# Windowed attention: low and high values side by side in one 512-column product

## The chip, the cores and the metric

The kernel runs on one core of one Trainium2 chip. The metric is device time in microseconds (us) of one execution. A profile of one execution shows every instruction of TensorE (PE, with its weight loads as PEld), VectorE (DVE), ScalarE (ACT), GpSimd (POOL) and the DMA queues.

## What is computed

The reference is an encoder trunk of two layers on 256 tokens of width 1024. Each layer is a feed-forward block, a mixer, and a second feed-forward block, each followed by a layer norm. The first layer's mixer is an mLSTM, the second's is the windowed attention that the change touches. Cut to what matters:

```
p = x @ w_in                              # 16 query heads, 4 key/value heads of 64
s = einsum('bnqkgd,bnskd->bnkgqs', q, kw) * (64 ** -0.5) - slopes * dist
s = where(valid, s, MASK_VALUE)           # |t - s| <= 128
m = maximum(max(s), sink)
pe = exp(s - m)
attn = pe / (sum(pe) + exp(sink - m))
o = einsum('bnkgqs,bnskd->bnqkgd', attn, vw)
return o @ w_out
```

Four query heads share one key/value head.

## The kernel before

**Stages.** Six stages follow each other: feed-forward, mLSTM, feed-forward, feed-forward, attention, feed-forward (`trunk_kernel`). All products are made from split numbers: each operand is written as a high part (rounded for TensorE, dtype `FR`) and a low part (what is left), and a product is high x high + high x low + low x high (`mm3`, line 617). `split_evac` (line 636) takes a result from PSUM in this way: ScalarE copies the high part, VectorE subtracts it from the result for the low part. Weights go the same road: `Weights.high` (ScalarE, `w_hi`) and `Weights.low` (VectorE, `w_lo`) split each piece of 128x1024; TensorE can use a piece only when both are done.

**Order.** The order of work is written out by hand (`manual_schedule`): each engine does its instructions in the order in which the program names them. `Paced` (line 65) wraps the engines and keeps modelled clocks (`pe`, `vec`, `act`); in the feed-forward stages a filler uses these clocks to choose where weight splits are put. In the attention there is no filler: `W.done(..., PU[st], True)` at line 1580 puts a fixed number of `w_hi` into each step (`PU` = 2, 1, 2, 1, 1, 0, 1, 2 for steps 3 to 10), and `W.lows()` at line 1584 the `w_lo` belonging to them.

**PSUM.** Two sets of four banks: `wbank` (name `pw`) and `ybank` (name `py`). A bank holds 128 x 512 numbers of 32 bits. A new `pw` tile takes the bank of the tile used longest ago, when all its readers are done.

**Attention** (`attn`, line 1335). Queries, keys and values are projected first; `qT`, `kT` hold transposed queries and keys, `va[t]` the values of 128 tokens. Then a loop of eleven steps `st` (line 1552) is a pipeline over eight pairs of heads j; pair j's two heads a = 0, 1 share one key/value head. In step st stand, in this order:

- `values(st - 3)` (line 1504): the sum of values weighted by probabilities, transposed: 128 rows (head a in rows 64a to 64a+63) by 256 queries. The result's high and low parts replace the queries in `qT[:, j]` (lines 1559, 1560; tiles `q_hi`, `q_lo`). In the prediction these two are d0 and d1.
- `rest` (two short exps `es` on ScalarE) and `scale(st - 1)` (line 1479): GpSimd divides pair st - 1's probabilities by their sums.
- a first part of the filling matmuls `work` (`FB[st]` of them): parts of the query projection in steps 0 to 3, of the output projection in steps 4 to 10.
- `turn(st - 2, 0, p0)` (line 1492): TensorE transposes pair st - 2's probabilities for the first 128 keys; ScalarE copies the high part (`pr`).
- `W.done`: the step's `w_hi` on ScalarE.
- `scores(st)` (line 1437), up to step 7: TensorE's scores; VectorE's four reductions (`sc`, with row minimum `nm`), with the low part of `pr` of the first 128 keys after the second; then `late`, which is `turn(st - 2, 1, p1)` for the other 128 keys; then four exps on ScalarE.
- `flush(2)`: the low part of the second `pr`; `W.lows()`: the step's `w_lo`, both on VectorE; and the rest of `work` on TensorE.

**values before.** `va[sb]` has five columns of 64 per key/value head: zeros, high, zeros, low, zeros. Twelve matmuls of 256 columns add up in a 128 x 256 result: for both blocks of keys sb and both heads a, (high values, high probabilities), (low, high), (high, low). The window `at` of 128 columns puts the values into the rows of head a and zeros into the other head's.

After the loop, `tail` (line 716) finishes the output projection; its first matmuls use chunk 7 of `qT`, which is `values(7)`.

Of the kernel before, what the change touches and what calls it, by code (L numbers as in the profile page):

```python
# [9 lines left out]
F32 = mybir.dt.float32  # L10
FR = mybir.dt.float32r
# [6 lines left out]
S = 256  # L18
# [170 lines left out]
class Weights:  # L189
# [134 lines left out]
    def low(self):  # L324

        nc = self.nc
        i, hi = self.half.pop(0)
        p = self.plan[i]
        k, scale, raw = p["k"], p["scale"], self.raw[p["word"]]
        lo = self.pool.tile([128, D], FR, name="w_lo", tag="w_lo", bufs=RING)  # L330
        if i == 0:
            for j in range(2):
                s_ = slice(j * 512, j * 512 + 512)
                nc.vector.tensor_sub(lo[:, s_], raw[:, s_], hi[:, s_].bitcast(F32))
        elif scale is None:
            nc.vector.tensor_sub(lo, raw, hi.bitcast(F32))
        else:
            nc.vector.scalar_tensor_tensor(lo, raw, scale(), hi.bitcast(F32), op0=OP.mult, op1=OP.subtract)
        self.parts[i] = (hi.rearrange("p (k f) -> p k f", k=k), lo.rearrange("p (k f) -> p k f", k=k))
        self.fresh = i  # L340
        sums = [(i, *sum_) for sum_ in self.after.get(i, ())]
        while sums and not isinstance(sums[0][2], int):
            self.transfer(*sums.pop(0)[1:])
        self.sums += sums
        self.drop(p["word"])
        self.load()
# [98 lines left out]
def trunk_kernel(ctx: ExitStack, tc: tile.TileContext, x, ffn_w_in, ffn_w_out, ln_g, ln_b, ml_w_in, ml_gate_b,  # L445
                 ml_norm_g, ml_w_out, at_w_in, at_sink, at_w_out, out):
    nc = Paced(tc.nc)
# [169 lines left out]
    def mm3(o, l, r, start, stop, onto=False):  # L617
        nc.tensor.matmul(o, l[0], r[0], start=start, stop=False, skip_group_check=onto)
        nc.tensor.matmul(o, l[0], r[1], start=False, stop=False, skip_group_check=onto)
        nc.tensor.matmul(o, l[1], r[0], start=False, stop=stop, skip_group_check=onto)  # L620

    def pair(p, *idx):
        return p[0][idx], p[1][idx]

    def wbank(shape=(128, 512)):
        return psum.tile(list(shape), F32, name="pw", tag="pw", bufs=4)
# [6 lines left out]
    def tok(t):  # L633
        return slice(t * 128, (t + 1) * 128)

    def split_evac(dst, src, scale=None, high=None, wait=False):
        if scale is None:
            (high or nc.scalar.copy)(dst[0], src)
            low = lambda: nc.vector.tensor_sub(dst[1], src, dst[0].bitcast(F32))
            if wait:  # L640
                W.when_ready(low, dst[0])
            else:
                low()
        else:
            nc.scalar.activation(dst[0], src, AF.Copy, scale=scale)
            nc.vector.scalar_tensor_tensor(dst[1], src, scale, dst[0].bitcast(F32), op0=OP.mult, op1=OP.subtract)
# [688 lines left out]
    def attn(l, n, pending, last):  # L1335
        with ExitStack() as ph:
            pool = ph.enter_context(tc.tile_pool(name="attn", bufs=1))
            tile_ = lambda shape, dt, name, **kw: pool.tile(shape, dt, name=name, tag=kw.pop("tag", name), **kw)

            def both(shape, name, bufs=1):  # L1340
                return tuple(tile_(shape, FR, name + e, bufs=bufs) for e in ("_hi", "_lo"))
# [24 lines left out]
                                        base=128, channel_multiplier=-sign)  # L1366
            dist = tile_([128, 2, S], F32, "dist")
            nc.gpsimd.tensor_add(dist, fwd, back)
            va = [tile_([128, 4, 5, 64], FR, f"v{t}") for t in range(2)]
            for t in range(2):  # L1370
                nc.gpsimd.memset(va[t][:, :, 0:5:2].bitcast(F32), 0.0)
            qT = both([128, 8, S], "q")
            kd, qd = [], []

# [2 lines left out]
            def proj(t, m):  # L1377
                ps = wbank()
                for k in range(8):
                    if t == 0 and m == 1 and k == PEND[bound[0] - 1]:  # L1380
                        pending()
                        W.done(0, PD[bound[0] - 1])
                    if 4 * m + k // 2 == len(pieces):
                        pieces.extend(W.take(1))
                    mm3(ps, pair(xT, A, k, tok(t)), pair(pieces[4 * m + k // 2], A, k % 2), k == 0, k == 7)
                    if t == 1 and k % 2:
                        W.done(W.used - 8 + 4 * m + k // 2 + 1, 1 if m == 0 and k < 4 else 0)
                if m == 0:
                    kv = ps.rearrange("p (a g d) -> p a g d", a=2, g=4)
                    kk = tile_([128, 4, 2, 64], F32, "kd", tag="sc", bufs=6)  # L1390
                    nc.scalar.copy(kk, kv[:, 0, :, None, :].to_broadcast([128, 4, 2, 64]))
                    split_evac((va[t][:, :, 1], va[t][:, :, 3]), kv[:, 1])
                    kd.append(kk)
                else:
                    qq = tile_([128, 4, 128], F32, "qd", tag="sc", bufs=6)
                    nc.vector.tensor_mul(qq.rearrange("p j (a d) -> p (j a) d", a=2),
                                         ps.rearrange("p (h d) -> p h d", h=8),
                                         qs_row[:, :, None].to_broadcast([128, 8, 64]))
                    qd.append(qq)
# [27 lines left out]
            sc, pr = {}, {}  # L1427
# [74 lines left out]
            lows, sums = [], {}  # L1502

            def values(j):
                p = wbank((128, S))
                terms = [(sb, a, e, f) for sb in range(2) for e, f in ((0, 0), (1, 0), (0, 1)) for a in range(2)]
                for n_, (sb, a, e, f) in enumerate(terms):
                    v = va[sb][:, j // 2].rearrange("p s d -> p (s d)")
                    at = 128 * e + 64 * (1 - a)
                    nc.tensor.matmul(p, v[:, at:at + 128], pr[j, sb][f][:, a], start=n_ == 0, stop=n_ == len(terms) - 1)  # L1510
                sums[j] = p
                for sb in range(2):
                    del pr[j, sb]
                    W.back(TAGS[2 + sb], 1)
# [17 lines left out]
            def parts(f_, *args):  # L1532
# [3 lines left out]
                return [lambda t=t, o=o: out_part(args[0], t, o) for t in args[1] for o in range(2)]  # L1536

            proj(0, 0)
            proj(0, 1)
            nc.scalar.preload_act_table(AF.Exp)  # L1540
            proj(1, 0)
            k_turn(0)
            q_turn(0)
# [8 lines left out]
            for st in range(11):  # L1552
                if st == 2:
                    gb = load_ln(lambda name: tile_([128, D], F32, name), l, n)
                if 0 <= st - 3 < 8:
                    values(st - 3)
                    o = sums.pop(st - 3)
                    d = pair(qT, A, st - 3)
                    nc.scalar.copy(d[0], o)
                    nc.vector.tensor_sub(d[1], o, d[0].bitcast(F32))  # L1560
# [36 lines left out]
    for j, (kind, l, i, n) in enumerate(stages):  # L1597
        last = j == len(stages) - 1
        bound[0] = j
        nc.filler = W.fill if kind == "ffn" else None  # L1600
        if kind == "ffn":
            pending = ffn(l, i, n, pending, last)
        elif kind == "mlstm":
            pending = mlstm(l, n, pending, last)
        else:
            pending = attn(l, n, pending, last)
# [29 lines left out]
```

## Time and profile before

| what | us |
|---|---|
| runs of the kernel before, median of 3 | 914.19 |
| lowest and highest | 912.9, 914.21 |
| span of the profiled execution, first to last instruction | 911.7 |
| median of the runs less that span | 2.5 |
| TensorE busy in the profiled execution | 902.5 |
| attention's steps 3 to 10, first `values` to last | 681.1 to 717.7 |

Of the profiled execution, the span is what the record holds; the median of the runs stands beside it. The profile is read in views: the page with its summary (busy times, the chain of work that ended last); stretches, which give for a window of time each engine's busy time, with the number of instructions, then the granted TensorE clock (1.00 is full speed), the DMA share and GB/s; the instructions in order of time (start, duration, engine, line, operation, output<-inputs, count, and in brackets how long the engine stood idle before and what ended it); groups of equal instructions (busy time in us, mean ns of one, idle time before them); and the view of one tile with what waited for it. Nearly all instructions pass through line 180, where `Paced` calls the engine, so they are told apart by tiles. Durations of neighbours overlap a little; the distance from start to start tells what an instruction costs its engine.

### The profile page before, as it was taken

How to read it: one execution, taken by the hardware profiler on the slowest of the kernel's cores; microseconds unless marked ns; L12 is line 12 of the kernel's file. 1: busy time of each engine (PE TensorE's matmuls, PEld its weight loads, DVE VectorE, ACT ScalarE, POOL GpSimd, SP SyncE). 2: the span in 40 equal slices, each digit the busy share in tenths (PEclk: the TensorE clock that was granted, in tenths of full speed). 3: DMA queues.
4: the chain of work that ended last, by engine and by line, in shares of the span. 5: the costliest groups of instructions: out<-in, count | busy, mean ns of one | idle time of the engine just before them, and what ended most of it. 6: DMA issues, size and time to landing. Idle time of an engine off the chain costs nothing.

```text
span 911.7 us, 12563 instructions
## 1 busy us (share of the span) xinstructions
PE 902.5 (99%) x4459; PEld 757.4 (83%) x4459; DVE 804.4 (88%) x971; ACT 573.1 (63%) x793; POOL 152.5 (17%) x192
## 2 busy tenths in 40 slices
PE   9999999999999999999999999999999999999996
PEld 7888888889988888888888888888898888888885
DVE  5999999886799898999888899998869889899886
ACT  5776777356664656776646676764569566676660
POOL 0111123113211011212011111110425301111110
PEclk9999999999999999999999999999999999999999
DMA  8999998546637898997868989986534587899851
GB/s 281 367 328 259 288 274 215 162 137 186 208 111 246 296 234 244 290 285 234 241 193 269 259 257 283 272 223 197 159 119 140 163 293 221 204 298 278 252 138 47
DMA packets 100703, 208.53 MB, mean 229 GB/s; under 512 B 6904, under 2 KB 21264, under 8 KB 100640
## 3 DMA queue, kind: packets, MB, share of 16 engines
q1 hardware_dynamic: 82368, 173.04, 54.2%
q0 software_dynamic: 17696, 33.65, 22.3%
q10 hardware_dynamic: 576, 1.05, 0.3%
q8 instruction: 35, 0.57, 0.3%
q14 instruction: 28, 0.23, 0.1%
HBM read 206.65 MB, written 1.05 MB: 228 GB/s over the span
## 4 chain that ended last, share of the span: by engine, by line
PE 98%; DVE 1%; DMA 0%; issue 0%; DVEq 0%
PE pw L180 64%; PE py L180 35%; DMA x<-in_x_dram 0%; DVE x L180 0%; DVE stats L180 0%; DVEq L1632 0%; DVE mv L180 0%; DVE rs L180 0%
## 5 line engine op out<-in xcount | busy, mean ns | idle before, releaser
L180 DVE TENSOR_TENSOR w_lo<-w_raw,w_hi 128x1024 fp32r<-128x1024 f32 (+1 forms) x213 | 255.2, 1219 | 26.6 <-ACT w_hi L180 24.8
L180 ACT CAST w_hi<-w_raw 128x1024 fp32r<-128x1024 f32 (+1 forms) x213 | 218.9, 1049 | 80.3 <-PE py L180 21.7
L180 DVE TENSOR_TENSOR w_lo<-s_raw,w_hi 128x1024 fp32r<-128x1024 f32 x192 | 228.6, 1219 | 18.3 <-ACT w_hi L180 18.2
L180 ACT CAST w_hi<-s_raw 128x1024 fp32r<-128x1024 f32 x192 | 196.6, 1054 | 58.4 <-PE py L180 23.3
L180 PE MATMUL pw<-w_hi,xT_hi 128*128 128x512 f32 x480 | 189.5, 396 | 0.0
L180 PE MATMUL pw<-w_hi,xT_lo 128*128 128x512 f32 x480 | 187.0, 391 | 0.0
L180 PE MATMUL pw<-w_lo,xT_hi 128*128 128x512 f32 x480 | 186.7, 390 | 0.0
L122 POOL DMA_DIRECT2D s_raw<-in_ffn_w_in_dram x64 | 77.4, 1211 | 484.1 <-DVE s_raw L180 226.3
L180 PE MATMUL py<-w_hi,h_hi 128*128 128x512 f32 x349 | 138.2, 396 | 0.0
L180 PE MATMUL py<-w_hi,h_lo 128*128 128x512 f32 x349 | 136.2, 390 | 0.0
L180 PE MATMUL py<-w_lo,h_hi 128*128 128x512 f32 x349 | 136.0, 390 | 0.0
L180 PEld LDWEIGHTS pw<-w_hi,xT_lo 128*128 128x128 f32 x480 | 90.0, 188 | 19.1
L180 PEld LDWEIGHTS pw<-w_lo,xT_hi 128*128 128x128 f32 x480 | 90.3, 188 | 18.6 <-DVE w_lo L180 1.2
L180 PEld LDWEIGHTS pw<-w_hi,xT_hi 128*128 128x128 f32 x480 | 90.1, 188 | 17.4 <-ACT w_hi L180 0.2
L180 PE MATMUL pw<-w_hi,S_hi 128*128 128x512 f32 x256 | 99.7, 390 | 0.0
L180 PE MATMUL pw<-w_lo,S_hi 128*128 128x512 f32 x256 | 99.7, 389 | 0.0
L180 PE MATMUL pw<-w_hi,S_lo 128*128 128x512 f32 x256 | 99.7, 389 | 0.0
L180 PEld LDWEIGHTS py<-w_hi,h_lo 128*128 128x128 f32 x349 | 65.5, 188 | 14.1
L180 DVE TENSOR_TENSOR s_raw<-s_raw,s_raw 128x1024 f32<-128x1024 f32 x64 | 76.8, 1219 | 0.3
L180 PEld LDWEIGHTS py<-w_lo,h_hi 128*128 128x128 f32 x349 | 65.7, 188 | 13.0
L180 PEld LDWEIGHTS py<-w_hi,h_hi 128*128 128x128 f32 x349 | 65.6, 188 | 12.7
L180 PEld LDWEIGHTS pw<-w_hi,S_lo 128*128 128x128 f32 x256 | 48.1, 188 | 10.0
(205 smaller groups left out, 1122.7 us busy)
## 6 DMA issues: line engine op xcount, KB each, us to landing
s_raw<-in_ffn_w_in_dram SPq DMA_DIRECT2D x96, 512.0 KB, 8.0
w_raw<-in_ffn_w_out_dram SPq DMA_DIRECT2D x88, 512.0 KB, 6.1
w_raw<-in_ffn_w_in_dram SPq DMA_DIRECT2D x64, 512.0 KB, 5.7
s_raw<-in_ffn_w_in_dram POOLq DMA_DIRECT2D x64, 512.0 KB, 8.3
w_raw<-in_ml_w_in_dram SPq DMA_DIRECT2D x24, 512.0 KB, 4.6
w_raw<-in_ffn_w_in_dram SPq DMA_DIRECT2D x32, 256.0 KB, 6.0
w_raw<-in_at_w_in_dram SPq DMA_DIRECT2D x12, 512.0 KB, 4.8
w_raw<-in_ml_w_out_dram SPq DMA_DIRECT2D x8, 512.0 KB, 4.1
```

The costliest lines, as they stand in the source:

```text
L122: self.nc.gpsimd.dma_start(ap, source, accum_op=OP.add)
L180: r = f(out, *args, **kw)
```

## The change

The values' columns are ordered low, high, zeros (three columns of 64 in place of five). A window of 128 columns from column 0 then holds low and high values side by side, and from column 64 high values and zeros. Each of the four matmuls has both heads' probabilities as its 512 columns: (low and high) with the high probabilities, (high and zeros) with the low probabilities, for two blocks of keys. The result is 128 x (2 heads x 256): rows 0 to 63 hold low x high + high x low, rows 64 to 127 hold high x high. Behind the matmuls, for each head, ScalarE copies the upper half into a new tile `o` and VectorE adds the lower half to it (for head 1 the halves change roles). In the prediction these four are c0, a0, c1, a1. d0 and d1 then read `o` in SBUF instead of PSUM.

```diff
-            va = [tile_([128, 4, 5, 64], FR, f"v{t}") for t in range(2)]
+            va = [tile_([128, 4, 3, 64], FR, f"v{t}") for t in range(2)]
             for t in range(2):
-                nc.gpsimd.memset(va[t][:, :, 0:5:2].bitcast(F32), 0.0)
+                nc.gpsimd.memset(va[t][:, :, 2].bitcast(F32), 0.0)
...
-                    split_evac((va[t][:, :, 1], va[t][:, :, 3]), kv[:, 1])
+                    split_evac((va[t][:, :, 1], va[t][:, :, 0]), kv[:, 1])
...
             def values(j):
-                p = wbank((128, S))
-                terms = [(sb, a, e, f) for sb in range(2) for e, f in ((0, 0), (1, 0), (0, 1)) for a in range(2)]
-                for n_, (sb, a, e, f) in enumerate(terms):
+                p = wbank((128, 2, S))
+                terms = [(sb, f) for sb in range(2) for f in range(2)]
+                for n_, (sb, f) in enumerate(terms):
                     v = va[sb][:, j // 2].rearrange("p s d -> p (s d)")
-                    at = 128 * e + 64 * (1 - a)
-                    nc.tensor.matmul(p, v[:, at:at + 128], pr[j, sb][f][:, a], start=n_ == 0, stop=n_ == len(terms) - 1)
-                sums[j] = p
+                    nc.tensor.matmul(p, v[:, 64 * f:64 * f + 128], pr[j, sb][f], start=n_ == 0, stop=n_ == len(terms) - 1)
+                o = tile_([128, S], F32, "o", bufs=2)
+                for a in range(2):
+                    r = slice(64 * a, 64 * a + 64)
+                    nc.scalar.copy(o[r], p[64 - 64 * a:128 - 64 * a, a])
+                    nc.vector.tensor_add(o[r], o[r], p[r, a])
+                sums[j] = o
```

## The prediction

> **What bounds the kernel now.** I read the page's busy line and its chain first, then the stretches of the attention stage, then that stage's instructions in order of time, engine by engine.
>
> ```profile
> PE 902.5 (99%) x4459; PEld 757.4 (83%) x4459; DVE 804.4 (88%) x971; ACT 573.1 (63%) x793; POOL 152.5 (17%) x192
> ...
> PE 98%; DVE 1%; DMA 0%; issue 0%; DVEq 0%
> ```
>
> TensorE is the bound of the whole: the chain that ended last runs on it for 98%. But these are averages over six stages, and the change lies in one. Two of the attention's eleven steps (step 4 and step 7 of the loop at line 1552), by the busy times of stretches (PE, PEld, DVE, ACT, POOL, clock):
>
> ```profile
> 685.96:691.50 5.54, 5.54 (x42) 4.66 (x41) 4.94 (x12) 5.32 (x17) 2.77 (x6) 1.00 0.32 106
> ...
> 702.50:708.00 5.50, 5.50 (x42) 4.67 (x41) 5.00 (x15) 4.87 (x16) 3.19 (x8) 1.00 0.54 171
> ```
>
> Here ScalarE is busy 4.87 to 5.32 and VectorE 4.94 to 5.00 of some 5.5 us: the three engines run level. ScalarE's 63% is the other stages' number. So the attention has almost no cover for more work on these two, and this decides the forecast.
>
> **The change, part by part: TensorE.** In the order of time, start and duration in us:
>
> ```profile
> 501.03 5.44 PE py L180 x24
> ```
>
> ```profile
> 681.10 1.60 PE L180 MATMUL pw<-pr,v 128*128 128x256 f32 x12
> 682.54 0.60 PE L180 MATMUL pw<-ident,sc 128*128 128x128 f32 x4
> ...
> 705.14 0.60 PE L180 MATMUL pw<-ident,sc 128*128 128x128 f32 x4
> 705.68 0.39 PE L180 MATMUL pw<-kT_hi,q_hi 64*128 64x256 f32 x2
> ...
> 706.59 0.66 PE L180 MATMUL pw<-ident,sc 128*128 128x128 f32 x4
> ...
> 708.47 1.80 PE L180 MATMUL pw<-pr,v 128*128 128x256 f32 x12
> ```
>
> The twelve matmuls of values took 682.54 - 681.10 = 1.44 us. Of 512 columns, 24 took 5.44, so 0.227 each and four 0.91. The change takes 0.53 us from TensorE per pair of heads, 8 x 0.53 = 4.2 us in all. That is the whole possible gain.
>
> **ScalarE and VectorE.** The result of values(j) now passes six instructions in a row where it passed two. Before: high copy d0, low subtraction d1. After: copy c0, add a0, copy c1, add a1, then d0, d1. Both engines work strictly in the order written, so each waits for the other with everything of its step queued behind. Step 7 before, on ScalarE and then on VectorE:
>
> ```profile
> 705.67 0.35 ACT L180 CAST q_hi<-pw 128x256 fp32r<-128x256 f32 x1
> 705.93 0.48 ACT L180 ACTIVATE es<-nm,sink 128x2 f32<-128x2 f32 x2
> 706.31 0.57 ACT L180 CAST pr<-pw 128x512 fp32r<-128x512 f32 x1
> 706.78 1.05 ACT L180 CAST w_hi<-w_raw 128x1024 fp32r<-128x1024 f32 x1
> 707.73 0.58 ACT L180 CAST pr<-pw 128x512 fp32r<-128x512 f32 x1
> ...
> 709.65 0.49 ACT L180 ACTIVATE sc<-sc,nm 128x256 f32<-128x256 f32 x1
> ...
> 710.14 0.50 ACT L180 ACTIVATE sc<-sc,nm 128x256 f32<-128x256 f32 x1
> ```
>
> ```profile
> 683.57 0.41 DVE L180 TENSOR_TENSOR q_lo<-pw,q_hi 128x256 fp32r<-128x256 f32 x1
> ...
> 689.53 0.48 DVE L180 SCALAR_TENSOR_TENSOR q_lo<-py,qs_col,q_hi 128x256 fp32r<-128x256 f32 x1
> 689.92 0.41 DVE L180 TENSOR_TENSOR q_lo<-pw,q_hi 128x256 fp32r<-128x256 f32 x1
> ...
> 695.00 0.43 DVE L180 TENSOR_TENSOR q_lo<-pw,q_hi 128x256 fp32r<-128x256 f32 x1 [0.18 <-ACT q_hi L180]
> ...
> 701.10 0.42 DVE L180 TENSOR_TENSOR q_lo<-pw,q_hi 128x256 fp32r<-128x256 f32 x1
> ...
> 706.05 0.42 DVE L180 TENSOR_TENSOR q_lo<-pw,q_hi 128x256 fp32r<-128x256 f32 x1 [0.18 <-ACT q_hi L180]
> 706.80 0.48 DVE L180 CUSTOM_DVE_ANT_0 sc<-pw,dist,neg_sink 128x256 f32<-128x256 f32 x1 [0.32 <-POOL sm L1485]
> ...
> 707.61 0.69 DVE L180 TENSOR_TENSOR pr<-pw,pr 128x512 fp32r<-128x512 f32 x1
> ...
> 709.02 0.69 DVE L180 TENSOR_TENSOR pr<-pw,pr 128x512 fp32r<-128x512 f32 x1
> 709.62 1.22 DVE L180 TENSOR_TENSOR w_lo<-w_raw,w_hi 128x1024 fp32r<-128x1024 f32 x1
> ...
> 711.02 0.43 DVE L180 TENSOR_TENSOR q_lo<-pw,q_hi 128x256 fp32r<-128x256 f32 x1 [0.18 <-ACT q_hi L180]
> ...
> 714.52 0.42 DVE L180 TENSOR_TENSOR q_lo<-pw,q_hi 128x256 fp32r<-128x256 f32 x1 [1.12 <-ACT q_hi L180]
> ```
>
> From start to start: d0 0.26, both es 0.38, a pr cast 0.47, w_hi 0.95, an exp 0.49; on VectorE two score reductions 0.81, a pr low part 0.60, w_lo 1.22 less the same overlap of 0.09, so 1.13. From one engine's end to the other's start 0.03 (705.67 + 0.35 to 706.05); I count 0.04.
>
> The new operations have no row, so they get bounds:
>
> ```profile
> L180 ACT CAST S_hi<-S 128x512 fp32r<-128x512 f32 x16 | 10.0, 623 | 15.2 <-DVE S L180 15.1
> ...
> L180 DVE DVE_READ_ACCUMULATOR2_ANT nm<- 128x1 f32 x32 | 2.7, 83 | 0.0
> ...
> L180 DVE TENSOR_TENSOR wt<-pw,wt 128x256 f32<-128x256 f32 x4 | 1.7, 414 | 0.0
> ```
>
> A copy of 64 partitions x 256 from PSUM lies between nothing and the 0.623 of 512 columns; I take 0.36, the q_hi cast of 256 columns. An add of 64 x 256 lies between 0 and 0.69 (512 columns); I take 0.42, the wt row with PSUM and SBUF in. d0 now reads SBUF: 0.35 to 0.62, I take 0.38; d1 stays 0.42.
>
> May c1 run while a0 runs? They touch other columns of one PSUM bank and other halves of o. The mLSTM stage has the same case: line by line, VectorE copies ucol from a bank and ScalarE reads ecol from its other columns, with nothing else between them.
>
> ```profile
> L180 ACT ACTIVATE ecol<-pw x1: 278/278/278, 213.5 to 213.5; 128x128 f32<-128x128 f32 x1
> its engine sat idle before it (us, times) until:
>   DVE ucol L180: 1.7, 1
> ```
>
> ScalarE stood idle until VectorE had read: the two are made to take turns on a bank. So I put c1 behind a0. [...]
>
> Count a step from a0's start, with one weight piece: a0 ends 0.42, c1 0.46 to 0.82, a1 0.86 to 1.28, d0 1.32 to 1.70, d1 from 1.74. ScalarE is free at 1.32 + 0.26 = 1.58 (before, 0.12 ahead of d1's start), VectorE at 1.74 + 0.33 = 2.07 (a 256-column subtraction by the 512 and 1024 ones: 0.60 - 0.27). Then VectorE: reductions to 2.88, pr low to 3.48, reductions to 4.29, pr low to 4.89, w_lo to 6.02. ScalarE: es 1.96, pr 2.43, w_hi 3.38, pr 3.85, first exp 4.34; the second waits for the last reduction's read-out (0.08) and hand-over, to 4.41, so three exps to 5.88, the next c0 to 6.24, next a0 at **6.28**. Before, step 7 took 711.02 - 706.05 = 4.97. With two pieces (steps 3, 5) the second pr cast ends 0.95 later, its low part runs 4.95 to 5.55, two w_lo to **7.81**, against 701.10 - 695.00 = 6.10.
>
> Start of a0 after, against d1's start before: step 3 683.57, the same. Step 3 has the two-piece 7.81 and one q_lo of a query projection more (0.39), so step 4 begins 691.77 (+1.85). Step 5: 698.05 (+3.05). Step 6: 705.86 (+4.76). Step 7: 712.14 (+6.09). Step 8: 718.42 (+7.40). Steps 8 and 9 have no scores: es and two pr casts, low parts ending at 3.87; the last matmul of values, which reads the second low part, is written 0.45 later (0.06 and 0.39, the duration of one of 512 columns); c0 at 4.35, a0 at 4.75, so step 9 at 723.17 (+8.65). There es is missing, but a w_hi follows the casts to 3.57 and its w_lo, to 4.74, stands in front of a0: step 10 at 727.91.
>
> TensorE covers none of it. Its own work of such a step is values 0.91, first transposes 0.54, scores 0.91, second transposes and output projection 708.47 - 706.59 = 1.88: 4.24, under 6.28; its last values matmul waits for the low part of the step before. The values bank goes to the second transposes (line 1575), which now wait for a1 (1.34) instead of d1; they are wanted by ScalarE only at 3.38. GpSimd's scaling follows es; it is busy 3.19 in step 7's stretch, so from 2.1 it ends about 5.3, and the transposes that read it come in the next step, whose reductions start at 6.28 + 2.07. No DMA moves; the smaller memset (POOL, line 1371) lies long before.
>
> ```profile
> 718.51 0.42 DVE L180 TENSOR_TENSOR q_lo<-pw,q_hi 128x256 fp32r<-128x256 f32 x1
> ```
>
> ```profile
> 719.12 0.39 PE L180 MATMUL py<-w_hi,q_hi 128*128 128x512 f32 x1
> ```
>
> After step 10 the output projection's tail begins with chunk 7, at 719.12 before. It needs d0: 727.91 + 1.70 + 0.06 = 729.67. **TensorE is 10.5 us late**, and from there to the end it has no gap to win any back. Span 911.7 + 10.5 = 922.2. The median of the runs is 914.19, 2.5 above the profiled span; with that, **924.7 us**.
>
> **The rivals.**
>
> *All is hidden, faster.* If ScalarE and VectorE took the six instructions in their idle time, TensorE would keep its 4.2: 914.19 - 4.2 = 910.0. The 98% chain speaks for it. The point from which it decides is the room of step 7: its two-engine loop before is by the same count 4.56 of 4.97 (0.33 + 0.81 + 0.60 + 0.81, 0.12 to the exps, 3 x 0.49, d0 and hand-over 0.42), so 0.4 us, and the change lengthens it by 1.7. 5%.
>
> *c1 beside a0.* If the two reads are allowed together, d0 starts at 0.79 rather than 1.32. Eight steps x 0.53 = 4.2 less: 920.5. For it: they read different columns and write different halves of o. Against: the ecol row, where that was so too. 10%.
>
> *The following stage is planned anew.* Paced (line 65) counts the changed instructions in its own clocks, and in the last feed-forward stage these choose when a w_hi or w_lo is written. One pair misplaced costs at most its 1.05 + 1.22 = 2.3 us where TensorE runs gapless: 925 to 929. 6%.
>
> *The clock drops.* TensorE would stand some 2 us of each step. Its clock was 1.00 in both stretches above, but there it never stood. At half clock its 4.24 would be 8.48, 2.2 over the step, and 1.5 over in the light ones: 5 x 2.2 + 3 x 1.5 = 15.5 more, 940. [...] 4%.
>
> **How the numbers follow.** Forecast 74%, with its own 922.5 to 927.0: the new operations' bounds, nearest rows taken, are worth some 0.25 us a step either way, 2 in all. c1 beside a0 10%, new plan 6%, clock 4%, hidden 5%, and 1% that gain and loss cancel. The range takes in most of the second and third: **920.0 to 928.5**. What a measurement of this kernel can tell from no change is about 0.2%, 1.8 us. Faster 5%, same 1%, slower 94%.
>
> **What would show it.** Right: four values matmuls of about 0.23 apart with a wait before the last; a0's starts 6.3 and 7.8 apart in steps 6 and 5; c1 starting just behind a0's end; ScalarE idle until VectorE's o; chunk 7 some 10 us later, all after it shifted alike. Wrong: c1 inside a0 (then 920.5); a0's steps under 5 us (then the gain); a clock under 1.00; gaps of TensorE in the last feed-forward.

## The result, and the profile after

| what | before | after |
|---|---|---|
| median of 4 runs each, us | 913.78 (912.9 to 914.21) | 926.45 (925.72 to 927.24) |
| span of the profiled execution, us | 911.7 | 924.2 |

The changed kernel takes 1.0141 times as long, with a 95% interval of 1.0127 to 1.0155: 12.7 us more by the medians, 12.5 by the spans. The prediction had 924.7 in a range of 920.0 to 928.5.

The page of the changed kernel, its busy line and the head of its chain:

```profile
PE 903.5 (98%) x4395; PEld 751.6 (81%) x4395; DVE 812.1 (88%) x987; ACT 580.7 (63%) x809; POOL 151.6 (16%) x192
...
PE 91%; DVE 6%; ACT 2%; issue 1%; POOL 0%; DVEq 0%; ACTq 0%; POOLq 0%
```

TensorE has 64 matmuls less, but its busy time did not fall. One reason is in the trace of step 7: a matmul next to a wait is counted with its full 0.4 to 0.5 us (717.86, 0.50, below), one in a running row adds only 0.23 (from 715.05 to the next at 715.28). What changed is the chain: 98% of it lay on TensorE, now 91%, and VectorE and ScalarE have 8%. Stretches of the changed kernel, steps 6 and 7, each from one a0 to the next (columns as before):

```profile
706.16:712.70 6.54, 5.13 (x22) 4.09 (x24) 5.54 (x15) 5.51 (x16) 3.06 (x6) 0.74 0.51 160
712.70:719.25 6.55, 5.20 (x33) 3.68 (x32) 5.55 (x14) 5.51 (x16) 3.06 (x6) 1.00 0.30 80
```

No engine fills these 6.54 us any more: VectorE and ScalarE are busy 5.5 each, TensorE 5.2. Three partly idle engines and a longer step are the sign of taking turns. Step 7 of the changed kernel in order of time, ScalarE first, then VectorE:

```profile
711.69 0.50 ACT L180 ACTIVATE sc<-sc,nm 128x256 f32<-128x256 f32 x1
...
712.30 0.37 ACT L180 COPY o<-pw 64x256 f32<-64x256 f32 x1
713.15 0.36 ACT L180 COPY o<-pw 64x256 f32<-64x256 f32 x1 [0.48 <-DVE o L180]
714.00 0.41 ACT L180 CAST q_hi<-o 128x256 fp32r<-128x256 f32 x1 [0.49 <-DVE o L180]
```

```profile
712.70 0.41 DVE L180 TENSOR_TENSOR o<-o,pw 64x256 f32<-64x256 f32 x1
713.54 0.43 DVE L180 TENSOR_TENSOR o<-o,pw 64x256 f32<-64x256 f32 x1 [0.43 <-ACT o L180]
714.44 0.42 DVE L180 TENSOR_TENSOR q_lo<-o,q_hi 128x256 fp32r<-128x256 f32 x1 [0.47 <-ACT q_hi L180]
714.90 0.48 DVE L180 CUSTOM_DVE_ANT_0 sc<-pw,dist,neg_sink 128x256 f32<-128x256 f32 x1
...
717.73 1.46 DVE L180 TENSOR_TENSOR w_lo<-w_raw,w_hi 128x1024 fp32r<-128x1024 f32 x1
```

The brackets alternate: 0.48 for VectorE's o, 0.43 for ScalarE's, 0.49, 0.47. Each of the last four instructions of the six (c1, a1, d0, d1) waits for the one before it on the other engine. From a0 to the first reduction of scores pass 714.90 - 712.70 = 2.20 us, in which VectorE works 1.26. Over all eight pairs, in the groups of VectorE (busy, mean ns | idle before, and what ended it), the changed kernel and then the one before:

```profile
L180 DVE TENSOR_TENSOR o<-o,pw 64x256 f32<-64x256 f32 x16 | 6.7, 417 | 5.0 <-ACT o L180 4.8
L180 DVE TENSOR_TENSOR q_lo<-o,q_hi 128x256 fp32r<-128x256 f32 x8 | 3.4, 425 | 3.8 <-ACT q_hi L180 3.8
```

```profile
L180 DVE TENSOR_TENSOR q_lo<-pw,q_hi 128x256 fp32r<-128x256 f32 x8 | 3.4, 420 | 1.7 <-ACT q_hi L180 1.7
```

VectorE has 6.7 us of adds more, and 5.0 + 3.8 - 1.7 = 7.1 us more of idle time ahead of these instructions. TensorE of the changed kernel in the same step 7, and then the start of the output projection's chunk 7:

```profile
714.12 0.63 PE L180 MATMUL pw<-ident,sc 128*128 128x128 f32 x4 [0.69 <-DVE o L180]
...
717.86 0.50 PE L180 MATMUL pw<-pr,v 128*128 128x512 f32 x1 [0.61 <-DVE pr L180]
...
731.01 0.50 PE L180 MATMUL py<-w_hi,q_hi 128*128 128x512 f32 x1 [1.11 <-ACT q_hi L180]
```

The second transposes wait for a1, the fourth values matmul for VectorE's low part of `pr`, and chunk 7 for d0. It starts at 731.01 instead of 719.12: 11.9 us late, of the span's 12.5.

### The profile page after: what moved, and what is told of

It is laid out like the page before. It is cut to its first block, busy times and chain, and to the rows that moved or that the text cites. A ratio compares the mean times of both kernels' runs of the same rounds, so it can differ in the third digit from the quotient of the medians.

```text
span 924.2 us, 12467 instructions
## 1 busy us (share of the span) xinstructions
PE 903.5 (98%) x4395; PEld 751.6 (81%) x4395; DVE 812.1 (88%) x987; ACT 580.7 (63%) x809; POOL 151.6 (16%) x192
## 4 chain that ended last, share of the span: by engine, by line
PE 91%; DVE 6%; ACT 2%; issue 1%; POOL 0%; DVEq 0%; ACTq 0%; POOLq 0%
PE pw L180 60%; PE py L180 31%; DVE w_lo L180 2%; DVE sc L180 1%; ACT w_hi L180 1%; DVE pr L180 1%; DVE o L180 1%; DVE x L180 1%; ACT o L180 0%; DVE stats L180 0%; ACT pr L180 0%; ACT sc L180 0%; DVE q_lo L180 0%; ACT q_hi L180 0%; POOL rs L700 0%
## 5 line engine op out<-in xcount | busy, mean ns | idle before, releaser
L180 PEld LDWEIGHTS py<-w_hi,h_hi 128*128 128x128 f32 x349 | 65.6, 188 | 12.7
L180 PEld LDWEIGHTS pw<-w_lo,S_hi 128*128 128x128 f32 x256 | 48.0, 188 | 10.0
```

The source lines that it names most:

```text
L180: r = f(out, *args, **kw)
```

## The experiments

Two theories stood against each other after the result. **Chain:** the whole loss is the evacuation, that is, taking the result out of PSUM, with its six instructions on two engines that work in order, and the shorter matmuls bring nothing. **Split account:** the matmuls do bring their 4.2 us, and the evacuation costs some 17. A third question was what within the evacuation costs: the added work, the turns on one PSUM bank, or what is queued behind the waiting instructions.

### Where did the gain go?

The changed kernel's matmuls alone. The two halves are not added, and the second head's result is not used:

```diff
-                o = tile_([128, S], F32, "o", bufs=2)
-                for a in range(2):
...
-                sums[j] = o
+                sums[j] = p[:, 0]
```

> The four matmuls of 512 columns without the adding behind them: d0 and d1 read the first head's half of the bank as it stands, so the sum of the halves and the second head's result are left out. Theory (the six-instruction evacuation makes the 12.5 us): the loss is gone and only part of TensorE's 4.2 us comes out, because steps 6 and 7 were already paced by a loop through VectorE (scores, reductions, low part, last values matmuls) that this does not shorten: 911 to 913, against 913.8 before. Rival (TensorE is the bound and its work counts in full): 909.6. Second rival (512-column matmuls themselves are the loss): over 920.

Measured: 913.02, against 913.39 before; ratio 0.9997 (0.9988 to 1.0006). The 4.2 us do not appear; at most 1.1 us of them fit the interval. Of this kernel, TensorE in one step in order of time, the VectorE instruction that it waits for, and the chain from 681 to 740 us by line (then the same chain of the kernel before):

```profile
693.52 0.84 PE L180 MATMUL pw<-pr,v 128*128 128x512 f32 x3
694.83 0.50 PE L180 MATMUL pw<-pr,v 128*128 128x512 f32 x1 [0.46 <-DVE pr L180]
```

```profile
694.08 0.69 DVE L180 TENSOR_TENSOR pr<-pw,pr 128x512 fp32r<-128x512 f32 x1
```

```profile
by line: PE pw L180 30.8%; PE py L180 27.8%; DVE pr L180 8.9%; DVE sc L180 6.0%; ACT w_hi L180 5.7%; issue 5.4%; ACT pr L180 5.3%; DVE w_lo L180 3.8%; ACT sc L180 3.0%; ACT es L180 1.5%; ACT q_hi L180 1.1%; DVE nm L180 0.7%; DVE q_lo L180 0
```

```profile
by line: PE pw L180 57.0%; PE py L180 43.1%
```

The low part ends at 694.77 and the last matmul starts at 694.83. TensorE comes to it earlier than before and stands: its saving turns into a wait for VectorE. A chain that is 100% TensorE, as before, says only that TensorE was never kept waiting. It does not say that the others had room: here their results were ready only just in time, which that chain does not show.

Is it that one wait alone? The last of the four matmuls (low probabilities of the second block of keys) is left out, and for a fair comparison the same is left out of the kernel before (its last two):

```diff
-                terms = [(sb, f) for sb in range(2) for f in range(2)]
+                terms = [(sb, f) for sb in range(2) for f in range(2)][:3]
...
-                sums[j] = o
+                sums[j] = p[:, 0]
```

> The matmuls alone as in e1, and of the four the last one left out (the low probabilities of the second block of keys), so that values waits for no low part of the step just before; besides what e1 leaves out, this term is missing from the result. e1 gave no gain: 913.0 with 913.4 before. Theory (TensorE's 4.2 us became a wait of the last values matmul for VectorE's low part): with that wait gone the gain comes out: 909 to 911. Rival (the gain is lost elsewhere, in the two-engine loop of ScalarE and VectorE): 912 to 913.

```diff
-                terms = [(sb, a, e, f) for sb in range(2) for e, f in ((0, 0), (1, 0), (0, 1)) for a in range(2)]
+                terms = [(sb, a, e, f) for sb in range(2) for e, f in ((0, 0), (1, 0), (0, 1)) for a in range(2)][:10]
```

> The kernel before with its last two values matmuls of 256 columns left out (the same term as in e8, missing from the result), as the measure for e8: it says what taking the wait away is worth alone. Theory: TensorE has 0.24 us less a step and the steps 6 and 7 lose some 0.3 of waiting: 911 to 912.5, that is 1 to 2 us over e8. Rival (the wait was worth nothing): 913.4; or (the wait alone is all): the same as e8.

Measured, against 913.81: 911.68 with the wide matmuls, ratio 0.998 (0.9971 to 0.999), and 912.13 with the narrow ones, 0.9982 (0.9973 to 0.9991). The first lay between the two theories' ranges. The difference of the pair is 0.4 us, within their intervals: even without that wait nothing measurable of the saving comes out. In the first of the two, TensorE then waits elsewhere:

```profile
690.70 0.66 PE L180 MATMUL pw<-ident,sc 128*128 128x128 f32 x4 [0.65 <-DVE q_lo L180]
...
710.20 0.77 PE L180 MATMUL pw<-ident,sc 128*128 128x128 f32 x5 [0.54 <-POOL sc L1489]
```

The transposes wait for VectorE's d1 (the bank) and for GpSimd's scaling. So when TensorE's own work gets shorter it meets more than one wait: the loop of VectorE, ScalarE and GpSimd runs at nearly TensorE's pace. Which part of that loop would have to become shorter for the 4.2 us to come out was not tried.

### Where did the loss come from?

The evacuation alone: the kernel before with its twelve matmuls, and the four instructions in front of d0 put on its 128 x 256 result. The sums are not attention's:

```diff
+                o = tile_([128, S], F32, "o", bufs=2)
+                for a in range(2):
+                    r = slice(64 * a, 64 * a + 64)
+                    nc.scalar.copy(o[r], p[64 - 64 * a:128 - 64 * a])
+                    nc.vector.tensor_add(o[r], o[r], p[r])
-                sums[j] = p
+                sums[j] = o
```

> The kernel before with its twelve matmuls of 256 columns, and the six-instruction evacuation of the change put behind them on its one 256-column result: the matmuls are the old ones, and the sum of shifted rows it makes is not the attention's result. Theory (ScalarE and VectorE taking turns pace every step, TensorE waits): the same as the change, 925 to 927.5, since TensorE's extra 0.53 us a step lies in its waits. Rival (TensorE's work counts too): 926.4 + 4.2 = 930.7.

Measured: 925.93, ratio 1.0139 (1.0122 to 1.0155), as the whole change. The groups of VectorE in this kernel:

```profile
L180 DVE TENSOR_TENSOR o<-o,pw 64x256 f32<-64x256 f32 x16 | 6.7, 416 | 5.1 <-ACT o L180 4.9
```

Busy and idle time are within 0.1 of those of the changed kernel. With it and the first experiment the two halves of the change add up: nothing for the matmuls, all of the loss for the evacuation. The split account falls.

The order of the four changed: both copies, then both adds.

```diff
                 for a in range(2):
                     r = slice(64 * a, 64 * a + 64)
                     nc.scalar.copy(o[r], p[64 - 64 * a:128 - 64 * a, a])
+                for a in range(2):
+                    r = slice(64 * a, 64 * a + 64)
                     nc.vector.tensor_add(o[r], o[r], p[r, a])
```

> The change with the order c0, c1, a0, a1: same work, two hand-overs between the engines fewer. Theory (the waits of the turns count, not only the work): from c0's start the high copy d0 comes at 1.45 us instead of 1.72, so 0.27 us a step, eight steps, 2.1 less: 924.3. Rival (only the added busy time counts): unchanged, 926.4.

Measured: 925.04, ratio 1.0132 (1.0116 to 1.0147), which overlaps the change's interval: by its time, this is open. The trace, step 7 on ScalarE and VectorE, says why so little came:

```profile
711.81 0.74 ACT L180 COPY o<-pw 64x256 f32<-64x256 f32 x2
713.47 0.41 ACT L180 CAST q_hi<-o 128x256 fp32r<-128x256 f32 x1 [0.92 <-DVE o L180]
```

```profile
712.58 0.85 DVE L180 TENSOR_TENSOR o<-o,pw 64x256 f32<-64x256 f32 x2 [0.43 <-ACT o L180]
```

a0 starts at 712.58, behind the end of both copies (711.81 + 0.74). I had expected it beside c1. From c0's start to d0's pass 1.66 us, and 1.70 in the changed kernel (712.30 to 714.00): only two hand-overs fewer.

Each head's result in a bank of its own (eight matmuls of 256 columns):

```diff
-                p = wbank((128, 2, S))
+                ps = [wbank((128, S)), wbank((128, S))]
...
+                    for a in range(2):
+                        nc.tensor.matmul(ps[a], v[:, 64 * f:64 * f + 128], pr[j, sb][f][:, a], ...)
...
-                    nc.scalar.copy(o[r], p[64 - 64 * a:128 - 64 * a, a])
-                    nc.vector.tensor_add(o[r], o[r], p[r, a])
+                    nc.scalar.copy(o[r], ps[a][64 - 64 * a:128 - 64 * a])
+                    nc.vector.tensor_add(o[r], o[r], ps[a][r])
```

> The change with each head's result in a bank of its own, by eight matmuls of 256 columns (0.95 us where four of 512 take 0.91): c1 need not wait for a0 any more. Theory (the bank makes c1 wait): d0 comes 0.53 us earlier in each of eight steps, 4.2 less: 922.2, with c1 starting inside a0. Rival (c1 waits for a0 for another reason, such as the shared tile o): unchanged, 926.4, c1 still behind a0. Second rival: six tiles a step on four banks hold the scores back, over 927.

Measured: 922.33, ratio 1.0098 (1.0083 to 1.0113). Step 7 of this kernel, ScalarE and VectorE:

```profile
710.50 0.76 ACT L180 COPY o<-pw 64x256 f32<-64x256 f32 x2
711.80 0.41 ACT L180 CAST q_hi<-o 128x256 fp32r<-128x256 f32 x1 [0.55 <-DVE o L180]
```

```profile
710.90 0.87 DVE L180 TENSOR_TENSOR o<-o,pw 64x256 f32<-64x256 f32 x2
```

Now a0 starts at 710.90 while c1 runs (c0 and c1 go through from 710.50 to 711.26 without a break), and d0 follows c0 by 1.30 us rather than 1.70. With a bank for each head c1 runs beside a0, with a shared one it does not. The shared bank is shown as the cause of that turn (a `pw` tile fills one bank here, so tile and bank are not told apart; the shared `o`, which stayed, is not the cause). Over eight pairs it is worth 3.5 to 4.1 us: the medians differ by 926.45 - 922.33 = 4.1, by 3.7 if each is taken against the kernel before as timed beside it, and chunk 7 starts at 727.51 instead of 731.01.

The scaling left out on GpSimd, since `w_lo` beside it took 1.46 us instead of 1.22 (the probabilities are then not divided by their sums):

```diff
-                for t in range(2):
-                    for a in range(2):
-                        nc.gpsimd.tensor_scalar(sc[j, t][:, a], sc[j, t][:, a], sm[:, t, a:a + 1], 1.0, ...)
```

> The change without GpSimd's scaling of the probabilities, so the results are not normalised. In the changed kernel the w_lo of a step of one piece took 1.46 us where others take 1.22, while GpSimd scaled. Theory (the two share something when both read and write SBUF): these w_lo take 1.22, and the steps of one piece stay within 0.1 us, since ScalarE's exps end at the same time: 925.5 to 926.4. Rival (the w_lo is long for another reason): still 1.46. Second rival (GpSimd's slowing of VectorE is a large part of the loss): under 925.

Measured: 925.72, ratio 1.0127 (1.0112 to 1.0142). The `w_lo` of step 7 in order of time, and the next a0:

```profile
718.02 1.22 DVE L180 TENSOR_TENSOR w_lo<-w_raw,w_hi 128x1024 fp32r<-128x1024 f32 x1
719.55 0.41 DVE L180 TENSOR_TENSOR o<-o,pw 64x256 f32<-64x256 f32 x1 [0.31 <-ACT o L180]
```

`w_lo` is 0.24 shorter, and the next a0 waits 0.31 for c0 instead: the steps stay at 6.52 to 6.53. ScalarE's side of the loop is as long as VectorE's.

### Can the loss be avoided?

All instructions stay, but d0 goes behind `w_hi` and d1 behind the second low part of `pr`, so that of the turns within a step only the adds' wait for the copies is left (both copies come first, as above; in steps 8 and 9 d0 goes behind the second copy of `pr`, and in step 10 d0 and d1 stay where they were):

```diff
-                    nc.scalar.copy(d[0], o)
-                    nc.vector.tensor_sub(d[1], o, d[0].bitcast(F32))
+                    highs = lambda o=o, d=d: nc.scalar.copy(d[0], o)
+                    lasts = lambda o=o, d=d: nc.vector.tensor_sub(d[1], o, d[0].bitcast(F32))
...
+                        if highs is not None and st < 8:
+                            highs()
                         turn(st - 2, 1, p1)
...
                 flush(2)
+                if lasts is not None:
+                    lasts()
```

> The change with c0, c1, a0, a1 in this order and the split d0, d1 moved to a later place of the same step: d0 behind the step's w_hi on ScalarE, d1 behind the second low part on VectorE. All instructions stay, none is taken away; only the standing about between them goes. Theory (the in-order waits are the loss, the added work alone nearly fits): steps of one piece 5.15 to 5.4 us instead of 6.54, of two pieces 6.7 instead of 7.9: 916 to 918.5. Rival (the added busy time of ScalarE and VectorE is the loss): 925 to 926.4.

Measured: 919.42 against 913.86; ratio 1.0058 (1.0041 to 1.0075), a little over the range of my theory and far from the rival. VectorE of this kernel in a step with one weight piece:

```profile
709.60 0.85 DVE L180 TENSOR_TENSOR o<-o,pw 64x256 f32<-64x256 f32 x2 [0.35 <-ACT o L180]
710.49 0.48 DVE L180 CUSTOM_DVE_ANT_0 sc<-pw,dist,neg_sink 128x256 f32<-128x256 f32 x1
...
713.31 0.41 DVE L180 TENSOR_TENSOR q_lo<-o,q_hi 128x256 fp32r<-128x256 f32 x1
713.65 1.22 DVE L180 TENSOR_TENSOR w_lo<-w_raw,w_hi 128x1024 fp32r<-128x1024 f32 x1
715.20 0.41 DVE L180 TENSOR_TENSOR o<-o,pw 64x256 f32<-64x256 f32 x1 [0.34 <-ACT o L180]
```

The first reduction comes 0.89 behind a0 instead of 2.20, and a step takes 715.20 - 709.60 = 5.60 instead of 6.54. So 926.45 - 919.42 = 7.0 of the 12.7 us were waiting in order: the same instructions in another order give it back. What is left, 5.6 us, goes with longer steps: 5.60 here against 4.97 before in step 7, where the two adds alone take VectorE 0.89. That this rest is nothing but the added work was not tried by itself.

d1 of that kernel put on GpSimd:

```diff
-                    lasts = lambda o=o, d=d: nc.vector.tensor_sub(d[1], o, d[0].bitcast(F32))
+                    lasts = lambda o=o, d=d: nc.gpsimd.tensor_sub(d[1], o, d[0].bitcast(F32))
```

> [...] Theory: VectorE is the longer engine only in steps of two pieces, so 0.4 us in two steps and little else: 1 less than the one before, 915 to 917.5; not under the kernel before's 913.8, since the loop through VectorE's low part and the last values matmul stays. Rival (VectorE paces all steps): 3 less. Second rival (GpSimd is slow enough to hold the next step's transposes): slower than the one before.

Measured: 920.09, ratio 1.0064 (1.0049 to 1.0079): no gain, where 1 us had been expected. GpSimd and VectorE of this kernel side by side:

```profile
705.97 0.74 POOL L1567 TENSOR_TENSOR q_lo<-o,q_hi 128x256 fp32r<-128x256 f32 x1
```

```profile
706.15 1.64 DVE L180 TENSOR_TENSOR w_lo<-w_raw,w_hi 128x1024 fp32r<-128x1024 f32 x1
```

`w_lo` begins inside GpSimd's subtraction and takes 1.64 us instead of 1.22. VectorE is rid of an instruction that cost it 0.34 and loses 0.42. This is the smaller part. From one a0 to the next, the steps with one piece take 5.64 to 5.66 us (5.59 to 5.60 with d1 on VectorE), and those with two pieces are 0.2 to 0.3 shorter. What takes the gain back is step 9, with 5.28 instead of 4.21: GpSimd came to step 8's subtraction only when its scaling had ended, and TensorE stood for it (near the second rival, but at a matmul of the output projection):

```profile
718.25 0.50 PE L180 MATMUL py<-w_hi,q_lo 128*128 128x512 f32 x1 [1.26 <-POOL q_lo L1567]
```

Last, the later d0 and d1 together with a bank for each head:

```diff
-                p = wbank((128, 2, S))
+                ps = [wbank((128, S)), wbank((128, S))]
...
+                    highs = lambda o=o, d=d: nc.scalar.copy(d[0], o)
+                    lasts = lambda o=o, d=d: nc.vector.tensor_sub(d[1], o, d[0].bitcast(F32))
```

> The two edits that helped, in one kernel with the full result: each head's values in a bank of its own and the split d0, d1 later in the step. In e5 the first add stood 0.35 us for the second copy, which read its bank. Theory: that wait goes, steps of one piece 5.25 instead of 5.6, a third of a us in each of eight steps: 916 to 917.5, still over the kernel before, since the added instructions stay. Rival (the six tiles a step on four banks hold it back): 919.4 or more. Second rival (beats the kernel before): under 913.

Measured: 921.11, ratio 1.0079 (1.0064 to 1.0094), worse than with one bank. Two waits of this kernel, on TensorE in step 7 and on VectorE in step 6:

```profile
710.84 0.38 PE L180 MATMUL pw<-kT_hi,q_hi 64*128 64x256 f32 x1 [0.61 <-DVE o L180]
```

```profile
706.02 0.48 DVE L180 CUSTOM_DVE_ANT_0 sc<-pw,dist,neg_sink 128x256 f32<-128x256 f32 x1 [0.96 <-PE pw L180]
```

With six tiles a step on `wbank`'s four banks, the scores wait for the adds to free a bank, and VectorE's reductions then wait for the scores. TensorE has the same wait of 0.60 in the kernel with two banks alone; there VectorE stands in front of its reductions for d0 in any case. No version with the wide product and the whole result came below the kernel before.

## Why the prediction was right, and which terms were off

**The cause.** Right: the six instructions in a row, on two engines without room. The evacuation alone gave 925.93. The rival "all is hidden" fell with the measured slower time, and the first experiment shows more than that: even with no evacuation at all the 4.2 us would not have come out. The working counted that gain as swallowed by the longer step; it had been swallowed by the old one too.

**c1 behind a0.** Right: 713.15 against a0's end at 713.11. The kernel with two banks shows the shared bank as the cause. The rival's price of 4.2 us was a little high, 0.53 a step where 0.40 came (d0 1.30 behind c0 instead of 1.70), since the two adds took 0.87 in a row and not 0.75.

**The step with one piece: 6.28 predicted, 6.54 measured.** This is the term that was too small. The start of a0 after, step by step, in the changed kernel (VectorE in order of time):

```profile
683.53 0.41 DVE L180 TENSOR_TENSOR o<-o,pw 64x256 f32<-64x256 f32 x1
691.76 0.40 DVE L180 TENSOR_TENSOR o<-o,pw 64x256 f32<-64x256 f32 x1
698.30 0.41 DVE L180 TENSOR_TENSOR o<-o,pw 64x256 f32<-64x256 f32 x1
706.16 0.41 DVE L180 TENSOR_TENSOR o<-o,pw 64x256 f32<-64x256 f32 x1
...
724.46 0.41 DVE L180 TENSOR_TENSOR o<-o,pw 64x256 f32<-64x256 f32 x1 [1.32 <-ACT o L180]
729.26 0.41 DVE L180 TENSOR_TENSOR o<-o,pw 64x256 f32<-64x256 f32 x1
```

Predicted were 683.57, 691.77, 698.05, 705.86, then 723.17 and 727.91. Step 3 came out at 8.23 (8.20 predicted) and step 5 at 7.86 (7.81); each of the steps 4, 6 and 7 is 0.26 longer. Two parts of it are in the rows of step 7. From d1's start to the first reduction I counted 0.33, with the overlap of neighbours in a running queue. It took 714.90 - 714.44 = 0.46: behind an instruction that waited, there was no overlap. And from the last exp's start to c0 I counted 0.49; it took 712.30 - 711.69 = 0.61. c0 began only behind the exp's read-out (712.09 + 0.19), where d0 of the kernel before began inside it (at 710.63, with the read-out from 710.54 for 0.18); why, the runs do not tell. Together 0.25. On VectorE's side `w_lo` took 1.46 instead of 1.22, which brought it to the same end, and the run without scaling shows that this alone changes nothing.

**Steps 8 and 9: 4.75 and 4.74 predicted, 5.21 and 4.80 measured.** In step 8 the next c0 starts at 724.05, 4.80 behind a0, where I had 4.35: the low parts ended as predicted (3.89, 3.87 counted), but the last values matmul and the hand-over behind it took 0.9 us rather than 0.45. In step 9, where `w_lo` stands in front of a0, this does not show. What the rest of the 0.9 is, the records do not tell.

**The tail: no term, and 0.6 us measured.** Chunk 7 was predicted at 729.67 and came at 731.01, 11.9 late in place of 10.5. The span is 12.5 longer, so "all after it shifted alike" was not quite so. TensorE at the start of the last feed-forward, the kernel before and then the changed one:

```profile
729.55 0.39 PE L180 MATMUL pw<-w_hi,xT_hi 128*128 128x512 f32 x1
...
730.00 0.39 PE L180 MATMUL pw<-w_hi,xT_lo 128*128 128x512 f32 x1
```

```profile
741.68 0.39 PE L180 MATMUL pw<-w_hi,xT_hi 128*128 128x512 f32 x1
...
742.40 0.50 PE L180 MATMUL pw<-w_hi,xT_lo 128*128 128x512 f32 x1
```

The first is 12.1 late, the third 12.4: before, they stood 0.45 apart, now 0.72, since the third waits for VectorE's `xT_lo` (its weight load, at 742.40, stood 0.53 for it). VectorE writes that from 741.67 on, before from 728.89: 12.8 later, more than TensorE's 12.1. So a tile that had come in time before now comes last. The other 0.2, between chunk 7 and the first of these, I did not trace further.

**The clock.** The rival's premise came true and its price did not. Half clock is in the kernel before too, at 0.50 from 910.0 to 911.7, behind its last matmul; that it would hold through every step no run shows. In the changed kernel it was 0.50 for some 3.4 us of step 6 and 1.00 in step 7: see below. **The new plan of the following stage** did not show: behind these 12.4 us the span ends 12.5 later, so at most 0.1 can have been lost there.

The terms 0.26 x 3, 0.08 in the two other steps with scores, 0.5 in steps 8 and 9 and 0.6 in the tail make 2.0 in all; the span was 2.0 over the predicted 922.2. These misses lie in one direction, so nothing cancelled to bring the forecast near. By the medians the miss is 1.8 (926.45 against 924.7).

## What to carry to other kernels

A chain of work that is all TensorE says that TensorE is never late; it does not say that a shorter TensorE makes the kernel shorter. Look at the other engines' loop in that stage, and if it is level, remove the work in question alone and see. Where an evacuation passes between two engines that work in order, count what is queued behind each wait, not only the instructions: here, putting two of the six later gave back 7.0 of 12.7 us, while a second PSUM bank for the same purpose helped alone (some 4 us) and hurt when combined with it, because banks ran short.

## What the runs showed of the hardware that was not expected

**The clock halved after a break of 1.7 us, in one kernel of three that had that break.** In the changed kernel's step 6 (TensorE in order of time):

```profile
707.57 0.64 PE L180 MATMUL pw<-ident,sc 128*128 128x128 f32 x4 [1.70 <-DVE o L180]
...
708.44 0.63 PE L180 MATMUL py<-w_lo,q_hi 128*128 128x512 f32 x1
708.86 0.63 PE L180 MATMUL py<-w_hi,q_lo 128*128 128x512 f32 x1
```

The pitch of 512 columns is 0.42 instead of 0.23, and the granted clock of the stretch is 0.74: it is 0.78 from 708.0 to 708.1, 0.50 from there to 711.4, 0.66 to 711.5 and then 1.00 again, so some 3.4 us at half. The break alone does not decide: the run without the scaling has the same break in the same step,

```profile
707.89 0.63 PE L180 MATMUL pw<-ident,sc 128*128 128x128 f32 x4 [1.70 <-DVE o L180]
```

and so has, with 1.67, the run of the evacuation alone, and in both the granted clock stayed at 1.00 from 705 to 713. What decides, the runs do not tell. The drop cost nothing: step 6 took 6.54 and step 7, at 1.00, 6.55, since TensorE had room in both, and step 6 of the run without the scaling, at 1.00, took 6.53. The clock rival had priced whole steps at half clock in every step, and the row of tenths on the profile's page, in which one digit stands for 23 us, shows nothing of this.

**Beside GpSimd's work, VectorE's `w_lo` took 1.46 us and more instead of 1.22.** `w_lo` took 1.22 us alone (728.12 in the changed kernel), 1.46 where GpSimd's scaling overlapped its start (717.73), and 1.22 again in the run without the scaling (718.02), which settles the cause; beside a GpSimd subtraction 1.64 (706.15). The scaling in the changed kernel's step 7, of which `w_lo` (from 717.73) meets the end:

```profile
716.27 1.84 POOL L1489 TENSOR_SCALAR sc<-sc,sm 128x256 f32<-128x256 f32 x4
```

In three cases the cost went with how long GpSimd's instruction still ran when `w_lo` started: 0.38 us were left in step 7 here and 0.24 were lost; with GpSimd's subtractions 0.56 were left and 0.42 lost, 0.73 and 0.59 (711.81, `w_lo` 1.81), each time 0.14 less than what was left.
